# The last states of a linear recurrence, stored once per layer in rows instead of sixteen times in columns

## The chip, the cores and the metric

One core of a Trainium2 chip runs the whole kernel in one launch. The metric is device time in microseconds (us): the median of several runs. The core's engines are PE (matrix products; PEld is its weight load), DVE (vector), ACT (activations), POOL (general purpose) and SP, which here does nothing but issue transfers. 16 DMA engines move the data.

## What is computed

Two trunk layers over 256 context and 1024 latent tokens of width 1024. In each layer an input projection feeds three mixers (windowed attention, neighbourhood attention and a recurrence called RG-LRU); their outputs are gated, merged and projected back. The change concerns one output of the recurrence. The recurrence has 512 channels and runs forward and backward over time:

```
h_t = a_t * h_prev + u_t              # a, u from gates on the convolved input
hf = linear_scan(a[0], u[0], h0, False)
hb = linear_scan(a[1], u[1], h0, True)
yc = (hf + hb) * silu(cg)
lru_state = stack([hf[:, -1], hb[:, 0]])   # the last context state of each direction
```

`lru_state`, of 2 layers x 2 directions x 512 channels, is the seventh output, `O[6]`.

## The kernel before

Activations lie with channels on the 128 partitions and tokens along the free axis, so the 512 channels of the recurrence are four blocks `f` of 128. The order of PE is written out by a planner (`Weave`): chains of work such as `lru` yield the time at which they may go on, `W.later(delay, fn)` puts a piece at a planned time (in ns), and gaps are filled with dense products of the input projection (`gt`, `cx`, later `k`, `q`, `v`). Every other engine, SP with its transfers among them, gets its order from the compiler's scheduler, and works strictly in that order.

In each layer the `lru` chain comes first, then `attention`. For a block `f`, `lru` does this:

- `conv(f)` (L614 to L616 on DVE) makes the convolved input `xc`, and splits it in a high part (`xh`, ACT L426) and a low part (`xl`, DVE L427), for products at full precision.
- The gate products `lg` on PE are taken from PSUM by ACT (L641 into `lR`, L643 into `lJ`), followed by elementwise work on ACT, POOL and DVE.
- The scans (DVE L684) run once for each direction `d` and segment (1024 latent tokens, 256 context tokens), and overwrite the buffer `R[d]` (profile name `lR`, three buffers).
- L686 then stores one column of `R[d]`, the last context state, to `O[6]`. The column has one 4-byte value on each of 128 partitions, so the store consists of 128 pieces of 4 bytes. It is issued by SP.
- L687 adds both directions in place (`nc.vector.tensor_add(R[0], R[0], R[1])`), and L688 writes the sum, 640 KB, to DRAM (`y_d`), from where the merge stage reads it back.

Because L687 overwrites `R[0]`, it has to wait until the store of L686 has read its column; a new block that takes over a `lR` buffer waits likewise. SP also issues the weight loads: `load_w` (L413) brings `wcx_r`, `wgt_r`, `wk_r` and others into a ring of two buffers, ACT casts them to a high part (L421), POOL makes the low part (L422), and only then can PE use them. `gate_evac` (L697, L698) copies a product out of PSUM to a tile of the ring `g2` (three buffers) and writes it to DRAM (`g_d`). `Keys.load_mask` (L898), `Keys.load_bias` (L905) and the load of the cached keys (`kc`, L778) stand at the start of `attention`.

Of the kernel before, what the change touches and what calls it, by code (L numbers as in the profile page):

```python
# [9 lines left out]
F32 = mybir.dt.float32  # L10
# [5 lines left out]
P = 128  # L16
# [173 lines left out]
def trunk(nc, tc, ctx, I, K, O):  # L190
    PSUM = bass.MemoryType.PSUM
    DRAM = bass.MemoryType.DRAM
    W = Weave()

    def pool(name, **kw):
        return tc.tile_pool(name=name, bufs=1, reuse_waits="tile", **kw)

    cp = ctx.enter_context(pool("const"))
# [4 lines left out]
    def ps_tile(tag, name):  # L203
        return pp.tile([P, 512], F32, tag=tag, name=name, bufs=PSB[tag])

    dma = nc.sync.dma_start
# [6 lines left out]
    def f32(ap):  # L213
        return ap.bitcast(F32)

    def mm(out, a, b, start, stop):
        nc.tensor.matmul(out, a, b, start=start, stop=stop)  # L217
        n = 1
        for d in b.shape[1:]:
            n *= d  # L220
        W.now += n / 0.6 + 3 if a.dtype == F32 else max(n * 17 / 38.4, 109) + 1

    def transpose(out, x, idn):
        nc.tensor.transpose(out, x, idn)  # L224
        W.now += 109
# [13 lines left out]
    ident, blk, ones_d, sel = cst[:, 0:128], cst[:, 128:256], cst[:, 256:384], cst[:, 384:386]  # L239
# [185 lines left out]
    def split(hi, lo, x):  # L425
        nc.scalar.copy(hi, x)  # L426
        nc.vector.tensor_sub(lo, x, f32(hi))  # L427
# [140 lines left out]


    def lru(l, H, rp):  # L570
        w_in = I["w_in"][l]
        dc, ct = dcol[l], colT[l]
        segs = ((0, 0, NLAT), (NLAT + 3, NLAT, NCTX))
        L = NTOK + 3
        tiles = {}

        def start(f):
            cx = rp.tile([P, NTOK + 6], F32, tag="cx", name=f"cx{l}_{f}")
            nc.vector.memset(cx[:, 0:2], 0.0)
            nc.vector.memset(cx[:, NLAT + 2:NLAT + 5], 0.0)  # L580
            nc.vector.memset(cx[:, NTOK + 5:NTOK + 6], 0.0)
            tiles["cx", f] = cx

        def cx_evac(f):
            def evac(ci, ps):
                c0, N = CHUNKS[ci]
                o = c0 + 2 if c0 < NLAT else c0 + 5
                nc.scalar.copy(tiles["cx", f][:, o:o + N], ps)
                if ci == 2:
                    W.mark(("cx", l, f), 1000)  # L590
            return evac

        for f in range(4):
            W.need.append((W.when(("H", l, 1), *([("conv", l, f - 1)] if f else [])),
                           job(w_in, O_CX + f * P, (0, 1, 2), lambda ci: H.cols(ci), cx_evac(f), f"cx{l}_{f}",
                               lambda f=f: start(f))))

        turn = [0]

        def conv(f):  # L600
            r = wp.tile([P, 4, P], F32, tag="wr", name=f"wl{l}_{f}", bufs=2)
            nc.gpsimd.memset(r, 0.0)
            for g, src in ((0, I["lru_wa"]), (1, I["lru_wx"])):
                for b in range(2):
                    dma(r[b * HD:(b + 1) * HD, 2 * g:2 * g + 2, b * HD:(b + 1) * HD],
                        src[l, :, 2 * f + b].rearrange("d k j -> k d j"))
            gh = rp.tile([P, 4, P], F32R, tag="gh", name=f"gh{l}_{f}", bufs=2)
            gl = rp.tile([P, 4, P], F32R, tag="gl", name=f"gl{l}_{f}", bufs=2)
            nc.scalar.copy(gh, r)
            nc.gpsimd.tensor_sub(gl, r, f32(gh))  # L610
            cx = tiles["cx", f]
            xc = rp.tile([P, L], F32, tag="xc", name=f"xc{l}_{f}", bufs=2)
            w = [ct[:, R_CW + 4 * j + f:R_CW + 4 * j + f + 1] for j in range(4)]
            nc.vector.tensor_scalar(xc, cx[:, 0:L], w[0], ct[:, R_CB + f:R_CB + f + 1], ALU.mult, ALU.add)  # L614
            for j in range(1, 4):
                nc.vector.scalar_tensor_tensor(xc, cx[:, j:j + L], w[j], xc, ALU.mult, ALU.add)  # L616
            xh = rp.tile([P, L], F32R, tag="xh", name=f"xh{l}_{f}")
            xl = rp.tile([P, L], F32R, tag="xl", name=f"xl{l}_{f}")
            split(xh, xl, xc)
            W.mark(("conv", l, f))  # L620
            tiles[f] = (gh, gl, xc, xh, xl)
            tiles["at", f] = W.now + T["cv"]

        yield W.when(("cx", l, 0))
        conv(0)
        for f in range(4):
            yield tiles["at", f]
            gh, gl, xc, xh, xl = tiles[f]
            R = [rp.tile([P, NTOK], F32, tag="lR", name=f"lR{l}_{f}_{d}", bufs=3) for d in range(2)]
            J = [rp.tile([P, NTOK], F32, tag="lJ", name=f"lJ{l}_{f}_{d}", bufs=2) for d in range(2)]  # L630

            def gate(g, d, ci):
                c0, N = CHUNKS[ci]
                o = c0 if c0 < NLAT else c0 + 3
                turn[0] += 1
                ps = ps_tile(LGB[turn[0] % len(LGB)], f"lg{l}_{f}_{d}_{g}_{ci}")
                for a, b, i in ((gh, xh, 0), (gh, xl, 1), (gl, xh, 2)):
                    mm(ps[:, :N], a[:, 2 * g + d], b[:, o:o + N], i == 0, i == 2)
                col = dc[:, 4 + 8 * g + 4 * d + f:5 + 8 * g + 4 * d + f]
                if g == 0:  # L640
                    nc.scalar.activation(R[d][:, c0:c0 + N], ps[:, :N], AF.Exp, bias=col, scale=-1.0)  # L641
                else:
                    nc.scalar.activation(J[d][:, c0:c0 + N], ps[:, :N], AF.Tanh, bias=col, scale=0.5)  # L643
            A, S = [], []

            for d in range(2):
                for ci in range(3):
                    gate(0, d, ci)
                    yield W.now + T["lg"]
            exp_ln(R[0])  # L650
            for d in range(2):
                nc.scalar.activation(R[d], R[d], AF.Ln, bias=1.0)
                nc.scalar.activation(R[d], R[d], AF.Exp, scale=-1.0)
                A.append(rp.tile([P, NTOK], F32, tag="lA", name=f"lA{l}_{f}_{d}", bufs=2))
                nc.scalar.activation(A[d], R[d], AF.Exp, scale=dc[:, 20 + 4 * d + f:21 + 4 * d + f])
                S.append(rp.tile([P, NTOK], F32, tag="lS", name=f"lS{l}_{f}_{d}", bufs=2))
                nc.gpsimd.tensor_tensor(S[d], A[d], A[d], ALU.mult)
            for d in range(2):
                nc.scalar.activation(R[d], R[d], AF.Tanh, scale=dc[:, 28 + 4 * d + f:29 + 4 * d + f])

                nc.vector.scalar_tensor_tensor(S[d], S[d], 1.0, R[d], ALU.add, ALU.mult)
            yield W.now + T["lr"]
            for d in range(2):
                for ci in range(3):
                    gate(1, d, ci)
                    yield W.now + T["lg"]
            if f < 3:
                yield W.when(("cx", l, f + 1))
                conv(f + 1)
            exp_ln(S[0])  # L670
            for d in range(2):

                nc.scalar.activation(S[d], S[d], AF.Ln, bias=tiny_c, scale=0.25)
                nc.scalar.activation(S[d], S[d], AF.Exp, scale=0.5)
                for o, c0, N in segs:
                    nc.vector.scalar_tensor_tensor(J[d][:, c0:c0 + N], J[d][:, c0:c0 + N], 1.0, xc[:, o:o + N],
                                                   ALU.add, ALU.mult)
                nc.vector.tensor_tensor(S[d], S[d], J[d], ALU.mult)
                st = ct[:, R_ST + 4 * d + f:R_ST + 4 * d + f + 1]
                for o, c0, N in segs:  # L680
                    a, u, h = A[d][:, c0:c0 + N], S[d][:, c0:c0 + N], R[d][:, c0:c0 + N]
                    if d:
                        a, u, h = a[:, ::-1], u[:, ::-1], h[:, ::-1]
                    nc.vector.tensor_tensor_scan(h, a, u, st if c0 < NLAT else 0.0, ALU.mult, ALU.add)  # L684
                e = NTOK - 1 if d == 0 else NLAT
                dma(O[6][0, l, d, f * P:(f + 1) * P].rearrange("(p o) -> p o", o=1), R[d][:, e:e + 1])  # L686
            nc.vector.tensor_add(R[0], R[0], R[1])  # L687
            dma(y_d[l][2][f], R[0])  # L688
            W.mark(("lru", l, f))
            yield W.now + T["le"]  # L690


    def gate_evac(dst, name):
# [673 lines left out]
    with tc.manual_schedule(engines={mybir.EngineType.PE}):  # L1367
# [84 lines left out]
        for l in range(DEPTH):  # L1452
# [3 lines left out]
            with pool(f"lru{l}", side=there) as rp:  # L1456
# [5 lines left out]
                W.run([lru(l, H, rp)] + ([ada_chain(late, rp)] if late else []))  # L1462
                W.settle()
            W.banks = ("d",)
            with pool(f"att{l}", side=there) as ap:
                W.run([attention(l, H, ap)])
                W.settle()
# [49 lines left out]
```

## Time and profile before

| what | value |
|---|---|
| median of 3 runs | 3245.91 us |
| lowest and highest run | 3237.86 and 3250.76 us |
| the profiled execution's own time | 3251.3 us |
| its span, first to last instruction | 3249.5 us |
| PE busy in the span | 3101.2 us, 95% |
| DVE, ACT, POOL busy | 55%, 52%, 30% |
| mean granted clock of PE | 0.977 of full speed |

The profile is of one execution. Its own time is 1.8 us above its span, and 5.4 us above the median. PE is the engine to watch: where it stands idle the program as a whole is late, and after an idle stretch it may be granted half its clock for a while. A DMA issue in the SP rows tells when the transfer was handed over, not when it landed; landing times are read from who waited for them.

### The profile page before, as it was taken

What the parts mean: (1) busy time and instruction counts of PE and PEld (TensorE: products, weight loads), DVE (VectorE), ACT (ScalarE), POOL (GpSimd) and SP (SyncE); (2) the same over time, 40 slices, a digit from 0 to 9 for tenths busy, and PEclk for the clock granted to TensorE, in tenths of its full rate; (3) what the DMA queues carried; (4) which work ended last, traced back from release to release, by engine and by line L of the source; (5) the groups of instructions that cost most, each with busy time, mean ns of one, the idle gap of its engine ahead of it and who ended that gap; (6) DMA issues with size and microseconds to landing.
All of it is one profiled execution on the core that took longest, in us unless ns stands there. A gap on an engine that the chain in (4) does not pass through costs nothing.

```text
span 3249.5 us, 48117 instructions
## 1 busy us (share of the span) xinstructions
PE 3101.2 (95%) x17419; PEld 2651.7 (82%) x17419; DVE 1787.8 (55%) x3275; ACT 1701.3 (52%) x3586; POOL 974.8 (30%) x815
## 2 busy tenths in 40 slices
PE   7897899999999999999999998999999999999999
PEld 5665688888888888888878787888888888888887
DVE  5563346756666665445462544666665666545541
ACT  5555445655556555533345683555655555554332
POOL 3543322212421221136333333222232222012633
PEclk9998899999999999999999999999999999999999
DMA  8556455445532332564442435455454333237543
GB/s 280 154 134 143 114 161 144 119 142 162 146 119 74 105 91 80 192 202 149 126 137 85 76 64 164 122 148 156 110 163 149 97 98 84 87 109 239 181 147 104
DMA packets 449707, 435.03 MB, mean 134 GB/s; under 512 B 77409, under 2 KB 370877, under 8 KB 448189
## 3 DMA queue, kind: packets, MB, share of 16 engines
q1 hardware_dynamic: 443484, 414.92, 44.4%
q0 software_dynamic: 5664, 16.83, 1.7%
q8 instruction: 137, 2.24, 0.3%
q14 instruction: 102, 0.83, 0.1%
q10 hardware_dynamic: 320, 0.21, 0.0%
HBM read 298.12 MB, written 137.29 MB: 134 GB/s over the span
## 4 chain that ended last, share of the span: by engine, by line
PE 71%; DVE 9%; ACT 6%; DMA 6%; issue 4%; POOL 3%; SPq 0%; ACTq 0%; DVEq 0%; POOLq 0%
PE gt L217 14%; PE sg L217 10%; PE po L217 7%; PE o L217 6%; PE pt L224 5%; PE q L217 5%; PE k L217 4%; PE v L217 4%; PE sc L217 3%; PE br L217 3%; PE sl L217 3%; PE cx L217 2%; POOL acc L1224 2%; DVE lR L684 1%; DMA out_dram<-lR 1%
## 5 line engine op out<-in xcount | busy, mean ns | idle before, releaser
L426 ACT CAST PT<-pt 128x512 fp32r<-128x512 f32 (+2 forms) x528 | 272.6, 536 | 343.2 <-PE pt L224 340.2
L427 DVE TENSOR_TENSOR PT<-pt,PT 128x512 fp32r<-128x512 f32 (+2 forms) x528 | 321.8, 621 | 104.7 <-ACT PT L426 102.0
L964 DVE TENSOR_REDUCE st<-sc 128x1 f32<-128x512 f32 x256 | 176.6, 690 | 314.2 <-PE sc L217 314.1
L217 PE MATMUL gt<-hhl,wgt_h 128*128 128x512 f32 x736 | 302.8, 411 | 2.9 <-ACT wgt_h L421 2.9
L217 PE MATMUL gt<-hhl,wgt_l 128*128 128x512 f32 x736 | 293.0, 398 | 9.1 <-POOL wgt_l L422 9.1
L217 PE MATMUL gt<-hll,wgt_h 128*128 128x512 f32 x736 | 291.6, 396 | 0.0
L422 POOL TENSOR_TENSOR wgt_l<-wgt_r,wgt_h 128x512 fp32r<-128x512 f32 x110 | 177.4, 1620 | 346.0 <-ACT wgt_h L421 314.4
L224 PE MATMUL pt<-cst,P 128*128 128x128 f32 x1856 | 270.8, 273 | 6.3 <-DVE Y L1054 3.8
L224 PEld LDWEIGHTS pt<-cst,P 128*128 128x128 f32 x1856 | 216.5, 140 | 16.8 <-issue 7.6
L217 PE MATMUL po<-z,wpo_h 128*128 128x512 f32 (+1 forms) x768 | 210.7, 362 | 7.6 <-ACT z L426 5.1
L217 PE MATMUL br<-yl,wbr_h 128*128 128x512 f32 (+1 forms) x576 | 204.4, 355 | 3.6 <-DVE yl L427 3.6
L986 ACT ACTIVATE P<-sc,st 128x512 f32<-128x512 f32 x256 | 175.4, 685 | 57.9 <-DVE st L980 57.4
L217 PE MATMUL br<-yh,wbr_h 128*128 128x512 f32 (+1 forms) x576 | 203.9, 354 | 0.8 <-DVE gl L1223 0.4
L217 PE MATMUL br<-yh,wbr_l 128*128 128x512 f32 (+1 forms) x576 | 204.0, 354 | 0.0
L217 PE MATMUL sc<-Kpast,Q 128*128 128x512 f32 x512 | 168.7, 411 | 28.4 <-ACT P L986 28.4
L422 POOL TENSOR_TENSOR wsg_l<-wsg_r,wsg_h 128x512 fp32r<-128x512 f32 x48 | 65.1, 1363 | 411.4 <-ACT wsg_h L421 313.2
L217 PE MATMUL o<-PT,Vpast 128*128 128x256 f32 x1024 | 175.8, 293 | 3.7 <-DVE Y L1048 2.1
L988 ACT ACTIVATE P<-sl,st 128x384 f32<-128x384 f32 (+1 forms) x320 | 171.1, 535 | 15.6 <-DVE st L976 15.3
L217 PEld LDWEIGHTS gt<-hhl,wgt_l 128*128 128x128 f32 x736 | 141.0, 192 | 42.4 <-POOL wgt_l L422 10.4
L217 PEld LDWEIGHTS gt<-hhl,wgt_h 128*128 128x128 f32 x736 | 141.4, 192 | 33.0 <-issue 5.5
L217 PEld LDWEIGHTS po<-z,wpo_h 128*128 128x128 f32 x768 | 137.8, 193 | 30.0 <-ACT z L426 6.0
L217 PEld LDWEIGHTS gt<-hll,wgt_h 128*128 128x128 f32 x736 | 141.6, 192 | 24.9 <-issue 0.5
(346 smaller groups left out, 8564.1 us busy)
## 6 DMA issues: line engine op xcount, KB each, us to landing
Q<-q_d SPq DMA_DIRECT2D x160, 256.0 KB
gl<-g_d SPq DMA_DIRECT2D x48, 640.0 KB
wgt_r<-in_w_in_dram SPq DMA_DIRECT2D x110, 256.0 KB
g_d<-tgt SPq DMA_DIRECT2D x92, 256.0 KB
wa<-in_w_ada_dram POOLq DMA_DIRECT2D x64, 256.0 KB, 4.4
wpo_r<-in_w_out_dram SPq DMA_DIRECT2D x64, 256.0 KB
yg<-y_d SPq DMA_DIRECT2D x24, 640.0 KB
yr<-s_d SPq DMA_DIRECT2D x24, 640.0 KB
```

Of the source, the lines that this page charges most:

```text
L217: nc.tensor.matmul(out, a, b, start=start, stop=stop)
L224: nc.tensor.transpose(out, x, idn)
L422: nc.gpsimd.tensor_sub(lo, r, f32(hi))
L426: nc.scalar.copy(hi, x)
L427: nc.vector.tensor_sub(lo, x, f32(hi))
L684: nc.vector.tensor_tensor_scan(h, a, u, st if c0 < NLAT else 0.0, ALU.mult, ALU.add)
L964: nc.vector.tensor_reduce(cm, psc, AX.X, ALU.min)
L986: nc.scalar.activation(pt[:, nl * P:(nl + 4) * P], psc, AF.Exp, bias=m, scale=-1.0, accum_out=sums[:, t, x, 1:2])
L988: nc.scalar.activation(pt[:, :nl * P], loc, AF.Exp, bias=m, scale=-1.0, accum_out=sums[:, t, x, 0:1])
L1224: (nc.vector if b == 0 and k >= KD - 2 else nc.gpsimd).tensor_add(z, z, g)
```

## The change

In `lru`, each scan's last column is copied by DVE into a small tile `fin` of 128 x 8 (one column for each direction and block) instead of being stored. Once per layer, 20 us of planned time into `attention`, `put_states` transposes that tile on PE to 8 x 128, copies it from PSUM to a `g2` tile, and stores it in 8 rows of 512 bytes. Sixteen stores become two.

```diff
     def lru(l, H, rp):
+        fin = cp.tile([P, 8], F32, name=f"fin{l}", tag="fin")
+        last_states.append(fin)
         w_in = I["w_in"][l]
...
                 e = NTOK - 1 if d == 0 else NLAT
-                dma(O[6][0, l, d, f * P:(f + 1) * P].rearrange("(p o) -> p o", o=1), R[d][:, e:e + 1])
+                nc.vector.tensor_copy(fin[:, 4 * d + f:4 * d + f + 1], R[d][:, e:e + 1])
             nc.vector.tensor_add(R[0], R[0], R[1])
             dma(y_d[l][2][f], R[0])
             W.mark(("lru", l, f))
             yield W.now + T["le"]
+
+
+    last_states = []
+
+    def put_states(l):
+        pt = ps_tile("t", f"fint{l}")
+        transpose(pt[:8, :P], last_states[l], ident)
+        t = cp.tile([P, 512], F32, tag="g2", name=f"fino{l}", bufs=3)
+        nc.vector.tensor_copy(t[:8, :P], pt[:8, :P])
+        dma(O[6][0, l].rearrange("d (f p) -> (d f) p", p=P), t[:8, :P])
...
             W.banks = ("d",)
+            W.later(20000, lambda l=l: put_states(l))
             with pool(f"att{l}", side=there) as ap:
```

## Rows read from the trace of the kernel before

**Rows 1.** The page's first part: busy time, share of span, instructions.
```profile
PE 3101.2 (95%) x17419; PEld 2651.7 (82%) x17419; DVE 1787.8 (55%) x3275; ACT 1701.3 (52%) x3586; POOL 974.8 (30%) x815
```

**Rows 2.** Waits of PE, whole span: us in total, times, longest.
```profile
PE lg L217 <- ACT lR L641: 17.0, 2, 14.2
PE k L217 <- ACT wk_h L421: 10.9, 1, 10.9
...
PE kct L224 <- DMA kc<-in_cache_kb_dram: 9.0, 1, 9.0
PE lg L217 <- DVE xl L427: 8.0, 3, 3.5
```

**Rows 3.** The tile lR: its stores; its engines' idle time before it, times.
```profile
L686 SPq DMA_DIRECT2D out_dram<-lR x16: 332/338/387, 176.5 to 1959.7; - x16
...
  DMA out_dram<-lR: 32.3, 8
```

**Rows 4.** The chain that ended last, in order of time: start, us, what.
```profile
176.50 8.95 DMA out_dram<-lR
...
225.14 4.57 DMA wcx_r<-in_w_in_dram
...
240.55 14.25 DMA wcx_r<-in_w_in_dram
...
351.99 9.74 DMA out_dram<-lR
...
1955.80 8.91 DMA out_dram<-lR
...
1969.98 5.12 DMA kc<-in_cache_kb_dram
```

**Rows 5.** Timeline of DVE, the last adds: start, us, line [idle before].
```profile
245.09 1.49 DVE L687 TENSOR_TENSOR lR<-lR,lR 128x1280 f32<-128x1280 f32 x1 [4.85 <-DMA out_dram<-lR]
...
361.82 1.49 DVE L687 TENSOR_TENSOR lR<-lR,lR 128x1280 f32<-128x1280 f32 x1 [9.28 <-DMA out_dram<-lR]
...
1964.80 1.49 DVE L687 TENSOR_TENSOR lR<-lR,lR 128x1280 f32<-128x1280 f32 x1 [5.14 <-DMA out_dram<-lR]
```

**Rows 6.** Timeline of SP around 237 us: the two stores of a block.
```profile
236.81 0.36 SPq L686 DMA_DIRECT2D out_dram<-lR  x1
...
239.63 0.34 SPq L686 DMA_DIRECT2D out_dram<-lR  x1
```

**Rows 7.** Timeline of ACT: casts of weights, and an evacuation.
```profile
187.81 0.62 ACT L421 CAST wgt_h<-wgt_r 128x512 fp32r<-128x512 f32 x1 [6.04 <-DMA wgt_r<-in_w_in_dram]
...
235.92 0.59 ACT L697 COPY tgt<-gt 128x512 f32<-128x512 f32 x1 [4.62 <-PE gt L217]
...
254.82 0.62 ACT L421 CAST wcx_h<-wcx_r 128x512 fp32r<-128x512 f32 x1 [16.45 <-DMA wcx_r<-in_w_in_dram]
```

**Rows 8.** Windows: us, busy (x) of PE, PEld, DVE, ACT, POOL, PEclk, DMA share, GB/s.
```profile
189.00:199.00 10.00, 9.93 (x32) 6.75 (x33) 0.17 (x1) 2.17 (x4) 0.77 (x1) 0.52 1.10 129
256.00:264.00 8.00, 7.92 (x28) 5.13 (x29) 0.79 (x5) 7.97 (x12) 3.80 (x4) 0.54 0.34 99
377.00:392.00 15.00, 13.09 (x42) 9.74 (x43) 1.31 (x2) 3.04 (x5) 6.75 (x6) 0.69 0.35 105
1800.00:1810.00 10.00, 7.74 (x27) 5.87 (x27) 7.05 (x8) 4.44 (x7) 2.81 (x2) 0.83 1.15 68
1975.10:1990.00 14.90, 14.85 (x65) 11.72 (x66) 6.41 (x9) 6.82 (x11) 6.87 (x6) 0.83 0.40 104
```

**Rows 9.** Groups of small operations, by form: busy us, mean ns.
```profile
L294 DVE TENSOR_SCALAR dcol<-colT 128x1 f32<-128x1 f32 x8 | 0.7, 142 | 0.0
L983 DVE TENSOR_TENSOR st<-st,sink 128x1 f32<-128x1 f32 x160 | 42.5, 265 | 2.8
L224 PE MATMUL colps<-cst,rows 88*128 88x88 f32 x2 | 0.6, 296 | 0.0
```

**Rows 10.** The page's groups: the evacuations of the attention's transposes.
```profile
L426 ACT CAST PT<-pt 128x512 fp32r<-128x512 f32 (+2 forms) x528 | 272.6, 536 | 343.2 <-PE pt L224 340.2
L427 DVE TENSOR_TENSOR PT<-pt,PT 128x512 fp32r<-128x512 f32 (+2 forms) x528 | 321.8, 621 | 104.7 <-ACT PT L426 102.0
```

## The prediction

> **What bounds the kernel now.** I read the page's busy shares first: PE works 95% of the span [rows 1], so time can come back only where PE stands still or runs at half clock. The second view is the list of PE's waits [rows 2]. Leaving out the attention's own, its three longest lie in the recurrence or at its end: 17.0 us in two waits for ACT's evacuation of a gate product (14.2 and so 2.8), 10.9 us for the weights of the first `k` product, 9.0 us for the cached keys. The third view is the tile `lR`: DVE and ACT together stood idle 32.3 us for the sixteen small stores [rows 3]. The fourth is the chain that ended last, for what stands between the stores and those four waits [rows 4], and the timelines of DVE, SP and ACT give the same places in detail [rows 5 to 7].
>
> The reader should see there that a store of 512 bytes takes 8.9 to 9.7 us from issue to release [rows 4], while a weight load of 256 KB landed in 4.57 us at 225 us. The DMA engines are at work all that time: share 1.15 at 68 GB/s around a pair of stores, against 0.35 at 105 GB/s elsewhere [rows 8]. And transfers queue behind them. At 237 us two stores go out at 236.81 and 239.63 [rows 6]; the first is over when the add may start, at 245.09 [rows 5], after 8.3 us; a second one of that length ends at 253.4, and the weight load issued after both at 240.55 lands 14.25 us later, at 254.80 [rows 4]. That is the sum of two stores in a row and little else.
>
> **The change, part by part.** *Sixteen stores removed.* Four places matter to PE.
>
> Place 1, layer 0, block 0. The store at 176.50 holds the weight load behind it; ACT waits 6.04 us for it, until 187.81 [rows 7], and PE the 2.8 us. With the store gone that load is there long before. Gain 2.8.
>
> Place 2, block 1. SP stands at the two stores in its order until the scans are over. Without them the load of `wcx_r` follows the `g_d` writes, whose data ACT has ready at 236.5 [rows 7]: issue near 237.7, landing after the 4.57 us of its undisturbed neighbour at 242.3, then ACT's cast and evacuation, 0.6 each, so PE goes on at 243.5 where it now goes on at 256.0 (254.82 and the same two steps). Gain 12.5; bounds 2.9 (only the earlier issue) and 14.2 (the whole wait).
>
> Place 3, the end of layer 0's recurrence. The add waits 9.28 us [rows 5]. Behind it on SP stand the write of `y_d`, eight small table transfers, the mask, the bias and then the `wk` weights that PE waits for. The whole queue moves up by the add's wait. Gain 9.3; at most the 10.9 that PE waits.
>
> Place 4, the end of layer 1's. The add waits 5.14 us; behind it on SP come `y_d`, mask, bias and `kc`, issued at 1969.98 [rows 4, 5]. Gain 5.1; at most 9.0, since `kc` no longer has two stores ahead of it.
>
> Together 29.7 us. The nine other blocks' waits are behind work that PE has anyway, and count nothing.
>
> *Clock.* After each of the four places PE ran at the lower of its two levels. From the granted clock [rows 8]: 0.52 over 10.0 us is 9.6 us at half rate, 4.8 lost; 0.54 over 8.0 gives 3.7; 0.69 over 15.0, less 1.9 idle, gives 3.7; 0.83 over 14.9 gives 2.5. That is 14.7 us at most. Rests of a few us remain at places 2 to 4, and gaps of at most 3.5 us [rows 2] were also followed by 0.83 [rows 8]. I take half: 7.3; bounds 0 and 14.7.
>
> *Sixteen copies added on DVE.* No row has this copy; the nearest, of one column, take 142 ns and 265 ns [rows 9]. I take 0.14, as the simpler one. Two stand in front of the add at each of the four places: 1.1 us; 2.1 at the other price. In the other blocks the adds and splits behind them are late by 0.3, which PE's dense products cover; uncovered it would be another 1.1.
>
> *Two transposes on PE.* The nearest row is 0.30 us [rows 9], so 0.6. *Two copies out of PSUM on DVE and two stores of 8 rows on SP*: nothing of this layer waits for them; they lie under the first products of the attention. The states are ready before PE gets there: the last scan ends before the products that PE waits for can start. SP stops at the new store until the copy is done; behind it stand loads for the next products. The store holds one of three `g2` buffers that ACT's evacuations use. If all cover were gone and it took as long as an old one, that is 8.9 us twice [rows 4], 17.8, my upper bound; below, 0, which I take, since the other two buffers go on.
>
> Sum: 29.7 + 7.3 - 1.1 - 0.6 = 35.3 us. The profiled execution took 3251.3 us, which gives 3216.0; its time is 5.4 us above the median, so 3211 us.
>
> One rule of the Trainium skill speaks against this. The page "DMA: Bandwidth & Descriptors" (section "Anatomy of one DMA — SWDGE (gpsimd) path") gives a transfer a fixed cost of about 2.0 us plus its bytes at 436 GB/s, fitted on another issuing path than SP's. The trace disagrees: 8.9 to 9.7 us for 512 bytes [rows 4]. By the page two stores could account for only an estimated 4 of the 14.25 us at place 2, which is the first rival below; the sum would be about 20 us.
>
> **Rivals.** *The loads stay slow.* The ring at these places also carries `g_d`, `wgt_r` and `y_d`; if these and not the stores made the load late, places 1 and 2 return only the earlier issue, 2.9 us, and the clock nothing. Places 3 and 4 are waits for the store itself and return 14.4. 17.3 - 1.7 = 15.6, so 3230 us. For it: other transfers are issued beside every pair of stores. Against it: share 1.15 at 68 GB/s, and the arithmetic of 8.3 and 14.25. Chance 0.24.
>
> *The low part falls behind the add.* With no wait for a transfer, the scheduler may put the add (1.49 us, [rows 5]) ahead of `xl`, for which PE already waits three times, 8.0 us [rows 2]. Six blocks by 1.49 are 8.9, and three new drops of the clock at some 1.7 (0.83 over 10.0 us) 5.1: 14 of the 35.3 go, 3225 us. Against it: `xl` stands earlier in the program. Chance 0.08.
>
> *Slower.* `put_states` takes a tile of PSUM's `t` ring of three, through which the attention's 528 transposes turn [rows 10]. If the shift by one makes the transposes of each of the 80 query groups wait for one eviction more, ACT's 0.54 and DVE's 0.62, that is 93 us lost, 3304; it decides from 0.44 us a group, where the 35.3 are used up. For it: ACT and DVE are in that loop at every step. Against it: one tile in 528, and the ring has no fixed partner. Chance 0.11, of which 0.09 is slower by over 0.5% and 0.02 within.
>
> **Numbers.** Over or under 0.5%, 16 us, is about what a measurement can tell here (the three runs spread by 13). The forecast has 0.57; its own range is 3193 (all bounds high: 2.8 + 14.2 + 10.9 + 9.0 + 14.7, less 1.7, is 49.9) to 3222 (clock 0, the dearer copies with no cover: 29.7 - 2.1 - 1.1 - 0.6 is 25.9, and 2 for the unseen). With the slow loads, 3230, and the store uncovered, 3229, the range is 3194 to 3238, which leaves out the slower case and a tail. Faster: 0.57, half of 0.24, and 0.06 of the 0.08, 0.75; same: 0.12 + 0.02 + 0.02, 0.16; slower 0.09.
>
> **What would show it.** Right: no wait of DVE before L687 for a transfer; PE's waits for `lR`, `wk_h` and `kc` down from 17.0, 10.9 and 9.0 to under 4, 4 and 5; fewer half-clock microseconds behind them; a DMA share that falls around the scans at the same GB/s. Wrong: PE waiting as long for `wcx_r` (first rival), more than 8.0 us for `xl` (second), or PE's waits in the attention up by tens of us (third).

## The result, and the profile after

The changed kernel takes 3198.77 us (median of 4 runs, 3196.05 to 3200.31), against 3241.89 us before (4 runs). The ratio is 0.9864 with a 95% interval of 0.9842 to 0.9886: 43 us faster, where 35.3 were forecast, and 12 us below the 3211 predicted.

The page of the changed kernel, its first part; it answers to [rows 1].

```profile
PE 3093.8 (97%) x17421; PEld 2642.1 (83%) x17421; DVE 1796.5 (56%) x3293; ACT 1707.7 (53%) x3591; POOL 974.9 (30%) x815
```

PE's busy time fell from 3101.2 to 3093.8 us. Its idle time fell from 148.3 (span 3249.5) to 104.7 (span 3198.5). So the two profiled spans differ by 51.0 us: 43.6 of idle time and 7.4 of the same work done at a better clock. That is 8 us more than the medians differ, since the execution profiled before, 3251.3 us, was slower than each of its four timed runs. PE's order of work is the same but for the two transposes; the scheduler also moved some work of DVE, ACT and SP.

PE's waits in the changed kernel (us in total, times, longest), which answer to [rows 2]:

```profile
PE lg L217 <- DVE xl L427: 5.5, 3, 1.8
...
PE k L217 <- ACT wk_h L421: 2.6, 1, 2.6
...
PE lg L217 <- DVE mod L362: 2.0, 1, 2.0
...
PE kct L224 <- DMA kc<-in_cache_kb_dram: 1.8, 1, 1.8
PE k L217 <- POOL wk_l L422: 1.6, 1, 1.6
```

The 17.0 us of waits for `lR` are gone, the 10.9 for `wk_h` are 2.6, the 9.0 for `kc` are 1.8. One small wait is new in this list: 2.0 us for `mod`, at 183.69.

The last add of layer 0, on DVE's timeline. The line number of the add, L687, has become L689.

```profile
318.87 0.27 DVE L688 COPY fin<-lR 128x1 f32<-128x1 f32 x2
319.06 1.48 DVE L689 TENSOR_TENSOR lR<-lR,lR 128x1280 f32<-128x1280 f32 x1
```

The add follows the copies at once, where it stood idle 9.28 us before [rows 5]. The new operations, from the view of the tile `fin`:

```profile
L688 DVE COPY fin<-lR x16: 120/141/157, 178.4 to 1907.0; 128x1 f32<-128x1 f32 x16
...
L224 PE MATMUL fint<-cst,fin x2: 271/272/273, 347.6 to 1915.4; 128*8 128x128 f32 x2
```

The windows that begin at the same product of PE as those of [rows 8], in time order; they lie 0.9, 23.7, 41.1, 44.0 and 57.0 us earlier:

```profile
188.10:198.10 10.00, 10.00 (x54) 7.57 (x53) 0.17 (x1) 9.22 (x11) 4.74 (x6) 1.00 0.74 204
232.30:240.30 8.00, 7.81 (x44) 5.45 (x43) 2.08 (x8) 5.71 (x8) 2.14 (x4) 1.00 0.73 226
335.90:350.90 15.00, 13.37 (x45) 10.04 (x46) 2.22 (x4) 3.04 (x5) 5.99 (x6) 0.77 0.34 99
1756.00:1766.00 10.00, 8.17 (x37) 6.33 (x36) 8.05 (x9) 5.90 (x10) 4.04 (x2) 1.00 0.28 102
1918.10:1933.00 14.90, 14.84 (x74) 11.81 (x75) 8.93 (x12) 8.16 (x14) 6.90 (x7) 1.00 0.49 129
```

The fourth is the one to read first: where the DMA share was 1.15 at 68 GB/s, it is 0.28 at 102 GB/s. More bytes move, and the engines are busy a quarter of the time. The prediction read the 1.15 as the DMA engines at work. The single packets in the trace of before say otherwise: between 1800 and 1810 us all 178 packets of 4 bytes, the stores' pieces among them, took 28 ns or less, while 59 of the 761 packets of 512 bytes, the size that a weight load consists of, took over 500 ns, and one 5.2 us, where their median is 27 ns. So the share counts packets of other transfers that were held up; in the changed kernel's window the longest packet of 512 bytes took 86 ns. The granted clock, the third number from the end, is full at places 1, 2 and 4, where it was 0.52, 0.54 and 0.83; at place 3, where a gap is left, it is 0.77 against 0.69.

### The profile page after: what moved, and what is told of

Its sections match the earlier page's. It is cut to its first block, busy times and chain, and to the rows that moved or that the text cites. A ratio compares the mean times of both kernels' runs of the same rounds, so it can differ in the third digit from the quotient of the medians.

```text
span 3198.5 us, 48113 instructions
## 1 busy us (share of the span) xinstructions
PE 3093.8 (97%) x17421; PEld 2642.1 (83%) x17421; DVE 1796.5 (56%) x3293; ACT 1707.7 (53%) x3591; POOL 974.9 (30%) x815
## 3 DMA queue, kind: packets, MB, share of 16 engines
q1 hardware_dynamic: 441212, 414.92, 43.6%
## 4 chain that ended last, share of the span: by engine, by line
PE 78%; DVE 9%; ACT 4%; DMA 3%; issue 3%; POOL 2%; SPq 0%; ACTq 0%; DVEq 0%; POOLq 0%
PE gt L217 15%; PE sg L217 10%; PE br L217 7%; PE po L217 7%; PE o L217 6%; PE pt L224 6%; PE q L217 6%; PE k L217 4%; PE v L217 4%; PE sc L217 4%; PE sl L217 3%; PE cx L217 3%; PE lg L217 2%; DVE lR L686 1%; POOL acc L1236 1%
## 5 line engine op out<-in xcount | busy, mean ns | idle before, releaser
L217 PE MATMUL sc<-Kpast,Q 128*128 128x512 f32 x512 | 168.5, 410 | 28.6 <-ACT P L998 28.6
```

## The experiments

Each was timed beside the kernel before. The table lists medians in us, and the ratio to the kernel before with its 95% interval.

| run | what is stored, and how | median | before | ratio | interval |
|---|---|---|---|---|---|
| the change | 8 rows of 512 bytes per layer | 3198.8 | 3241.9 | 0.9864 | 0.9842 to 0.9886 |
| e1 | 1 piece of 4 bytes per store | 3196.1 | 3240.0 | 0.9864 | 0.9842 to 0.9885 |
| e2 | every store twice | 3260.6 | 3240.0 | 1.0065 | 1.0042 to 1.0088 |
| e3 | 128 pieces from the small tile, SP | 3238.6 | 3240.0 | 0.9991 | 0.9979 to 1.0003 |
| e4 | 1024 pieces at once, late | 3209.4 | 3240.0 | 0.9898 | 0.9872 to 0.9925 |
| e5 | nothing | 3193.4 | 3240.6 | 0.9856 | 0.9842 to 0.9871 |
| e6 | 128 pieces from the small tile, POOL | 3234.4 | 3240.6 | 0.9984 | 0.9969 to 0.9998 |
| e7 | 128 pieces of 512 bytes | 3203.0 | 3240.6 | 0.9889 | 0.9873 to 0.9906 |
| e8 | 128 pieces of 4 bytes, 512 bytes apart | 3197.3 | 3240.6 | 0.9867 | 0.9853 to 0.9882 |
| e9 | 128 pieces of 4 bytes, 16 bytes apart | 3199.7 | 3239.5 | 0.9877 | 0.9855 to 0.9899 |
| e10 | 64 pieces side by side | 3225.8 | 3239.5 | 0.9957 | 0.9942 to 0.9971 |
| e11 | as the change, 180 us later | 3199.5 | 3239.5 | 0.9872 | 0.9855 to 0.9890 |
| e12 | 16 pieces side by side | 3204.1 | 3237.8 | 0.9894 | 0.9867 to 0.9922 |

**Is it the wait for the store, or the store's length?** In e1 each store is there, waited for, and in its old place on SP, but short.

```diff
-                dma(O[6][0, l, d, f * P:(f + 1) * P].rearrange("(p o) -> p o", o=1), R[d][:, e:e + 1])
+                dma(O[6][0, l, d, f * P:f * P + 1].rearrange("(p o) -> p o", o=1), R[d][:1, e:e + 1])
```

> The kernel before, but each of the sixteen stores writes only partition 0 of its column: one piece of 4 bytes instead of 128 (127 of 128 states are not written). Who waits for whom, and SP's order, stay as they were. Theory (the 128 pieces take some 8 us of the transfer queue, and everything else follows from that): the add's waits at the ends of the layers all but vanish, loads behind a store land in some 5 us; about 3205 us, 3198 to 3214 (SP still stands at the stores until the scans end, worth some 3 us in block 1 of layer 0). Rival (a store costs by being one: the wait until it has landed and SP's standing at it, whatever its pieces): 3230 to 3242.

3196.1 us. All of the gain comes from the store's length: the order of instructions is that of before on every engine, the add still has to wait for the store, and SP still stands at it until the scans end. In the time this standing doesn't show; in PE's waits it does, at place 2, where 3.1 us of the 14.2 for `lR` are left, close to the 2.9 that the prediction gave to the earlier issue.

**Is it the held buffer?** In e3 the columns go by way of the small tile, so the add doesn't wait; the stores are as long as before.

```diff
                 nc.vector.tensor_copy(fin[:, 4 * d + f:4 * d + f + 1], R[d][:, e:e + 1])
+                c = 4 * d + f
+                dma(O[6][0, l, d, f * P:(f + 1) * P].rearrange("(p o) -> p o", o=1), fin[:, c:c + 1])
...
-            W.later(20000, lambda l=l: put_states(l))
```

> The copies into the small tile are kept, but each column is stored from that tile at once, as before in 128 pieces; no transpose. So no buffer of the scans is held by a store, the pieces in the queue are as many as before. Theory (queue): the add waits no more, but loads behind the stores are as late as before, and PE waits for loads at three of the four places: 3220 to 3240, most likely 3228. Rival (the held buffer is what costs): 3196 to 3206, like the change.

3238.6 us: no gain clear of noise. Of e3, rows of the timelines of DVE and SP and, below, PE's waits (`bias_d<-t_d` are the small table transfers):

```profile
348.64 1.48 DVE L691 TENSOR_TENSOR lR<-lR,lR 128x1280 f32<-128x1280 f32 x1
```

```profile
351.94 10.75 SPq L1369 DMA_DIRECT2D bias_d<-t_d  x9
```

```profile
PE k L217 <- ACT wk_h L421: 8.3, 1, 8.3
...
PE lg L217 <- ACT lR L643: 7.8, 1, 7.8
...
PE kct L224 <- DMA kc<-in_cache_kb_dram: 7.2, 1, 7.2
```

The add runs the moment the scans end, and PE still waits 8.3, 7.8 and 7.2 us at places 3, 2 and 4, for loads. Before it was 10.9, 14.2 and 9.0, in an execution some 10 us slower than the one profiled here (3251.3 against 3241.5 us).

**Is it the queue?** e6 issues the same stores from POOL, and leaves SP's queue to the loads (the edit is that of e3 with `nc.gpsimd.dma_start`).

> The small tile's columns are stored at once, 128 pieces each, but issued by POOL, so that they go through another queue than the weight loads; no transpose. Theory (a load waits because it stands behind a store in its own queue): 3196 to 3210 us, POOL's own issue time included. Rival (the 16 DMA engines are shared, so the other queue changes nothing): 3228 to 3242, like the same stores from SP.

3234.4 us: better by 0.16%, with an interval of 1 to 10 us. PE's waits in e6 (`ada` is the product that uses the weights `wa`):

```profile
PE ada L348 <- DMA wa<-in_w_ada_dram: 18.6, 5, 7.1
PE k L217 <- ACT wk_h L421: 7.9, 1, 7.9
...
PE kct L224 <- DMA kc<-in_cache_kb_dram: 7.1, 1, 7.1
```

At places 3 and 4 `wk` and `kc`, on SP's queue, are as late as in e3, though no store stands in that queue: SP is held at the nine table transfers for 11.60 us there, against 10.75 in e3 and 6.15 in the changed kernel. So what the stores hold up is shared by both queues. At place 2 the queue did matter: SP no longer stands at the stores, the load goes out before them (at 231.12), and the wait for `lR` is gone. In its stead the weights `wa`, which POOL loads, are late: 18.6 us, where they cost PE 1.4 in the recurrence before. A part of that is POOL's own order, since POOL stands at the stores until the scans end, 11.7 us in three waits in layer 0. Issued by POOL a store took 8.1 us from issue to landing (the median of the sixteen, from 7.1 to 15.5), so it is as long as from SP.

**Which property of the store makes it long?** Five runs keep the order of before on every engine, and change only where the pieces go, how large they are or how many; the scratch `scr` is a tile in DRAM.

```diff
 # e8, and e9 with [P, 4]
+                scr = dp.tile([P, P], F32, name=f"scr{l}_{d}_{f}")
+                dma(scr[:, 0:1], R[d][:, e:e + 1])
 # e7
+                e0 = NTOK - P if d == 0 else NLAT
+                dma(dp.tile([P, P], F32, name=f"scr{l}_{d}_{f}"), R[d][:, e0:e0 + P])
 # e10 (64), e12 (16)
+                dma(O[6][0, l, d, f * P:f * P + 64].rearrange("(p o) -> p o", o=1), R[d][:64, e:e + 1])
```

> The kernel before, in the same order on every engine, but each store puts its 128 pieces of 4 bytes 512 bytes apart into a scratch in DRAM, where they lay side by side in one stretch of 512 bytes (the state output is not written). Theory (pieces that fall into one short stretch of DRAM are written one after the other, some 65 ns each, 8.3 us for 128): apart they go in parallel, and the time is that of one piece per store, 3194 to 3206 us. Rival (every 4-byte piece costs its time, wherever it goes): 3234 to 3244, like before.

> The kernel before, in the same order on every engine, but each store takes 128 columns instead of one and puts 128 pieces of 512 bytes, 64 KB, into a scratch in DRAM (the state output is not written). Theory (one short stretch): no two pieces share one, 3196 to 3208 us. Rival (the number of pieces): 3234 to 3250.

3197.3 and 3203.0 us, both in the theory's range. The same number of pieces, and in e8 of the same size, costs almost nothing if they don't lie side by side. That the pieces go to a scratch instead of the output isn't the reason: e2, below, stores side by side into a scratch, and there the add waits as long as before.

> The kernel before, in the same order on every engine, with the 128 pieces of 4 bytes 16 bytes apart in a scratch in DRAM, a stretch of 2 KB (the state output is not written). Theory with a stretch of 512 bytes: 32 pieces in each of four, which go in parallel, 2 to 3 us a store, 3196 to 3208. Rival (a stretch of 2 KB or more is the unit): 3234 to 3244; a unit of 64 bytes would give 3194 to 3200, which this run tells from 512 only by the landing times.

3199.7 us: 16 bytes apart is already enough, so the stretch in which pieces hinder each other is not as long as 2 KB. At the end of layer 0 a store is issued at 325.92 and the add starts at 327.76, 1.8 us later; that is less than the 2 to 3 us expected for a stretch of 512 bytes, but too near to rule it out.

> The kernel before, in the same order on every engine, but each store writes only the first 64 of its 128 states, side by side (the other 64 are left out). Theory (pieces in one short stretch are written one after the other): a store takes half as long, 4 to 5 us where it was 8.9 to 9.7, and the add at the end of layer 0 waits 4 us instead of 9.3; about 3214 us, 3203 to 3225. Rival (a fixed price as soon as several of the transfer engines write into one stretch): the same landing times, 3234 to 3244.

3225.8 us, just outside the range of the theory that the time goes with the pieces. The landing times tell why. These are rows from the end of layer 0: of the chain that ended last in e10 (64 pieces), then of DVE's timeline in e8 (apart) and in e12 (16 pieces):

```profile
344.29 7.38 DMA out_dram<-lR
```

```profile
326.46 1.49 DVE L688 TENSOR_TENSOR lR<-lR,lR 128x1280 f32<-128x1280 f32 x1 [0.95 <-DMA scr<-lR]
```

```profile
329.14 1.49 DVE L687 TENSOR_TENSOR lR<-lR,lR 128x1280 f32<-128x1280 f32 x1 [0.90 <-DMA out_dram<-lR]
```

From issue to release: 9.7 us with 128 pieces [rows 4], 7.4 with 64, and about 1.5 with 16 (issued at 327.69, add at 329.14) and with 128 apart (324.95, 326.46). So the time grows with the pieces side by side, but not in proportion.

> The kernel before, in the same order on every engine, but each store writes only the first 16 of its 128 states, side by side (the other 112 are left out). A store took 7.4 us with 64 pieces and 9.7 with 128 at the end of layer 0, and one piece was free. If there is a fixed price as soon as pieces side by side are more than one (the line through 64 and 128 starts at 5 us), 16 pieces take 5.6 us: 3212 to 3226 us. If the time goes with the pieces (7.4 / 64 each), 16 take some 2 us: 3194 to 3204.

3204.1 us, at the edge of the second answer; a fixed price from the second piece on is out.

**Twice the stores.** e2 adds to each store a second one, to a scratch of its own, with the pieces side by side: `dma(dp.tile([P, 1], F32, ...), R[d][:, e:e + 1])`.

> The kernel before, with every store of a column made a second time, to a scratch in DRAM: 256 pieces where there were 128. Theory (pieces go through the queue one after the other): a load behind a pair of stores is late by another 16 us, the add at a layer's end by another 8 to 16; four places together 35 to 65 us more: 3275 to 3310. Rival (stores overlap in the queue, the cost is the landing time of one): 3240 to 3255.

3260.6 us, between the two ranges. At the end of layer 0 four stores are issued one after the other, at 354.38, 354.77, 355.32 and 355.71. A row of DVE's timeline shows when the add could start, and a row of the chain how long the third store took:

```profile
364.31 1.49 DVE L688 TENSOR_TENSOR lR<-lR,lR 128x1280 f32<-128x1280 f32 x1 [9.38 <-DMA scr<-lR]
```

```profile
355.32 16.72 DMA out_dram<-lR
```

The add overwrites `R[0]`, which the first two stores read. It waits 9.38 us for the two, where it waited 9.28 for one: these two overlap, as the rival has it. The third takes 16.72 us where one took 9.7, and SP's table transfers wait for it: the later stores follow the first pair, as the theory has it. Only 20 us of all this reach the end, less than the 35 expected. The added stores also change the order on SP, ACT and DVE, so this is no clean measure of what a microsecond of store costs.

**One store of columns.** e4 keeps the gathering, and stores the tile without transpose, in 1024 pieces:

```diff
     def put_states(l):
...                                     # the five lines of the change are gone
+        dma(O[6][0, l].rearrange("d (f p) -> p (d f)", p=P), last_states[l])
```

> The changed kernel without transpose: the gathered tile of 128 x 8 is stored at the same place in one transfer of 1024 pieces of 4 bytes. Theory (pieces in the queue): 1024 pieces at 8.3 us per 128 are 66 us per layer in front of the first attention's loads; PE has work for only part of it: 3250 to 3330. Rival (what counts is one store instead of eight, and no held buffer): 3196 to 3206.

3209.4 us: neither. PE waits 12.4 us for `kc` in two waits (9.1 the longest) instead of 1.8, where one wait of 9.0 stood before. By the trace's records of completion the store landed 10.9 us after its issue in layer 0 and 11.1 in layer 1, little more than a store of 128 pieces. Its pieces fill eight rows of 512 bytes, and pieces that follow each other in the transfer lie in different rows; that the rows are worked on at the same time fits, but was not tried apart. So of the 43 us some 31 to 33 come from storing once per layer, and some 10 from the rows.

**The floor and the place.** e5 leaves the line out; e11 moves the rows' store from 20000 to 200000.

> The kernel before without any store of the states (the seventh output is not written). This is the floor for every way to store them. Theory: the change's copies, transposes and two stores cost 0 to 3 us, so 3194 to 3199. Rival (the change still pays a wait somewhere for them): under 3192.

> The changed kernel with its transposes and row stores 200 us of planned time into the attention instead of 20 us. If the 5 us between the change and the kernel without any store of states come from their place at the start of the attention, where PE, DVE and SP are busy with the first products: 3193 to 3197. Rival (they come from the sixteen copies, or are the runs' spread): 3196 to 3201.

3193.4 and 3199.5 us; the first lies just under the theory's range and above the rival's, the second in its rival's range. Storing the states costs the change some 5 us over storing nothing, with intervals that overlap, and the place is not where they come from. No way to store all states was measured to be faster than the change.

## Why the prediction was right, and where it was not

The gain came where the prediction looked for it, and the signs that it named came too: no add waits for a transfer, and PE's waits for `lR`, `wk_h` and `kc` are 0, 2.6 and 1.8.

**The places.** PE's idle time at the four places fell as follows: place 1, from 2.8 to 0 at the weights, but 0.8 to 2.0 at the wait for `mod` just before; place 2, from 14.2 to 0; place 3, from 10.9 + 1.9 to 2.6 + 1.6; place 4, from 9.0 to 1.8. That is 1.6, 14.2, 8.6 and 7.2, together 31.6, against 2.8, 12.5, 9.3 and 5.1, 29.7 in the sum. At place 2 more came back than expected because the load itself now goes out at 221.26, before the scans end; behind the stores' old place on SP, e1's 3.1 us would be left.

**The term that was too small** is the list of places itself: 43.6 us of idle time went, so 12 lie elsewhere, where the prediction said that the other waits "count nothing". (It speaks of nine other blocks; two layers have eight blocks in all, so there are four.) Some show: `xl` 8.0 to 5.5 and a wait of 2.2 for `cx` at 213 that is gone. The rest was not followed gap by gap, and part of it belongs to the execution profiled before, which was slower than its median.

**The clock.** Half of 14.7, 7.3, was taken; PE's busy time fell by 7.4. That these are so close is in part luck. The windows show the clock come back whole at three of the places, which by the prediction's own prices are 4.8, 3.7 and 2.5, together 11.0 and not half. A part is lost again: after the longer wait for `mod` at place 1 the granted clock is 0.55 from 184.8 to 187.8, where the same products ran at 1.00 before, and `lg` products of 0.40 us take 0.63. Where else the rest went was not followed.

**The step that failed** is the cause at places 3 and 4: "The whole queue moves up by the add's wait." The sizes came out near. And in the kernel before, the delay did go by way of that wait: the loads there weren't slow, only issued late. `wk` was cast 5.1 us after its issue (371.23 to 376.36), in the changed kernel 5.2 (330.07 to 335.24); `kc` landed after 5.1 us [rows 4], in the changed kernel PE goes on 6.0 us after its issue. But taking the wait away doesn't move the queue up. In e3, seen from the last evacuation of `gt` before the scans end, the write of `y_d` goes out 9.2 us earlier than before and `wk` only 2.9, because SP is now held at the table transfers (10.75 us for nine, against 5.95 for eight before). At place 4 SP is held 2.7 us by a store before it issues `kc`, which then takes 8.0 us. So PE's waits fell by 2.6 and 1.8 us of the 9.3 and 5.1 that this step gives to them, and the time by nothing clear of noise. What counts is how long the stores take: while they run, the loads are late by one way or another. The first rival rested on the same step, with its 14.4 us that "are waits for the store itself". It is refuted twice: by e3, which takes those waits away for no gain, and by e1, which leaves them, makes the stores short and gains everything.

**"Transfers queue behind them"** was half the matter. At place 2 twice 8.3 us fits the load's landing at 254.80, but two stores needn't follow each other: in e2 two issued together held the add no longer than one. And loads of another queue are late too (e6), so the stores hold something that the queues share.

**The range.** Its own low end, 3193, doesn't follow from its bounds: 49.9 us below the median of 3245.9 is 3196. The measured 3198.8 lies inside either way.

**The rule against it.** A store whose pieces lie 512 bytes apart took about 1.5 us (e8), one with 128 pieces side by side 9.7. The Trainium skill's page "DMA: Bandwidth & Descriptors" (section "Anatomy of one DMA — SWDGE (gpsimd) path"), with its 2.0 us, is near the first and far from the second. The prediction left room for the difference because the page's fit is for another issuing path than SP's; that is not the reason, since the stores that POOL issued in e6, on the path that the page is about, took 7.1 to 15.5 us. The section "Specifications" of the same page of the Trainium skill says that a transfer below 512 bytes is read, changed and written back; no run here shows that step, and in e8 small pieces alone cost nothing clear of noise (3197.3 us, against 3193.4 without any store of the states).

**The other rivals.** `xl` did not fall behind the add: PE's waits for it went down. The attention's transposes did not slow down: the waits of `sc`, `pt` and `o` are as they were, 28.6 us for `sc` against 28.4. The copies took 141 ns (0.14 taken), the transposes 0.27 (0.30).

**What stays open.** Why pieces side by side are slow: 16 take about 1.5 us, 64 take 7.4, 128 take 9.7, 128 with 16 bytes between their starts about 1.8. A conflict between the DMA engines over one short stretch of DRAM fits most of this, but 16 pieces, in a stretch of 64 bytes, were quick. That each engine hinders itself, with pieces of its own that follow each other side by side, fits too: dealt out over 16 engines, 16 pieces are one for each, and 64 are four. No run tells these two apart.

## What to carry to other kernels

A column of one value for each of 128 partitions, stored to consecutive addresses, was a slow transfer out of all proportion to its bytes, and it delayed the loads beside it, on its own queue and on the other; transpose it on the chip and store rows, or gather it and store once. When a profile shows an engine waiting for such a store, don't expect the time back from ending that wait: look for the loads that come late around it, whether they are issued late or land late, and at the DMA share against the GB/s. To tell a wait from its transfer, take the wait away and keep the transfer (e3), and shorten the transfer and keep the wait (e1).

## What the runs showed of the hardware that was not expected

- 128 pieces of 4 bytes took 8.9 to 9.7 us side by side in DRAM, about 1.5 us when 512 bytes apart, and 1.8 when 16 bytes apart; 16 pieces side by side took about 1.5. A run with 128 pieces of 512 bytes, 64 KB, lost little (3203.0 us, against 3197.3 for 4 bytes).
- 1024 such pieces in one transfer, over eight rows of 512 bytes, landed after 10.9 and 11.1 us, hardly later than 128 in one row.
- Two stores issued together held the add 9.38 us, one 9.28; a third, issued with them, took 16.72.
- Stores issued by POOL delayed SP's loads at the ends of the layers as much as SP's own stores did (7.9 and 7.1 us of PE's waits, against 8.3 and 7.2).
- While such stores ran, the DMA engines showed a busy share of 1.15 at 68 GB/s: packets of other transfers took up to 5.2 us, where their median is 27 ns.
